# Five slightly wider matmuls at the start of each feed-forward of a two-layer diffusion step

## The chip, the cores and the metric

The program runs on one core of a Trainium2 chip. The metric is the device time of one execution in microseconds; the median of three executions is given. Beside it there is one execution taken with the hardware profiler, which lists each instruction of each engine with its start and duration. PE is TensorE's matmuls, PEld its weight loads, DVE is VectorE, ACT is ScalarE, POOL is GpSimd, SP the engine whose queue issues all DMA transfers here.

## The reference

Two groups of 128 tokens each, a context group and a denoising group, go through two layers of width 2048. A layer is a mixer (latent attention and grouped-query attention in the first, differential attention in the second) and a gated feed-forward with a convolution over positions. The feed-forward, which the change touches, is

```
def conv_ffn(h, w_up, w_conv, b_conv, w_down):
    u = h @ w_up
    up = jnp.pad(u, ((0, 0), (1, 1), (0, 0)))
    u = up[:, :-2] * w_conv[0] + up[:, 1:-1] * w_conv[1] + up[:, 2:] * w_conv[2] + b_conv
    gate, val = u[..., :D_FF], u[..., D_FF:]
    return (jax.nn.silu(gate) * val) @ w_down
```

with D_FF = 5632. All inputs, weights and outputs are float32. Both groups use the same weights, and the kernel keeps their tokens side by side: a row of the activations has NT = 256 columns, 128 of each group.

## The kernel before

Activations lie with features on the 128 partitions and tokens along the free dimension. A product of float32 accuracy is made of three matmuls on rounded operands: each weight block is split by ScalarE and VectorE into a high part wh and a low part wl (`split`, L236, called from `Weights.chunk`, L274), each activation into a high and a low half. The operand hx holds for each of the 16 feature blocks k a row of 512 columns: 256 of the high half, then 256 of the low half.

`gemm` (L323) makes one chunk of output, 128 features by 256 tokens, in one PSUM bank of 512 columns taken from a pool of three, called acc. It walks the input blocks, 16 for an up-projection and 22 for half a down-projection, and for each issues wh times the high half, wh times the low half and wl times the high half. A weight load goes ahead of each matmul. The first matmul of a chunk clears the accumulator (start), the last closes it. So an up-projection chunk is 48 matmuls and a down-projection chunk 66, all 128x256. All of TensorE's instructions go through `placed` (L104, or L107 for transposes), so all have these lines in the profile and are told apart by their tiles.

The feed-forward (`ffn`, L1246) takes 88 up-projection chunks in turn (gate and value of each of the 44 feature blocks), in two halves of 44, each followed by 16 down-projection chunks that add to the residual. `conv` asks the local function product for a chunk. The first three chunks are `ready`: made before, by `modulated` (L666), from an operand that has not been normalised yet and has 258 columns instead of 256 (UW, two of them for the shift). The next four come from the list in_order: they are issued in a fixed order. The third of these four, chunk 5 when counted from 0, has a hook in its middle (turn): four transposes into a bank called misc, which end the computation of a modulation vector. From chunk 7 on in_order is empty and nothing stands between the chunks.

The order on each engine comes from a scheduler with a timeline simulation of its own. Weights come as tiles of 1 MB through SP's queue (raw), three of them in flight, and the split parts wh and wl have four buffers each.

Of the kernel before, what the change touches and what calls it, by code (L numbers as in the profile page):

```python
# [21 lines left out]
NT = 2 * T  # L22
# [32 lines left out]
LATE = 3  # L55

EARLY = (2, 5, 8, 11, 13)
SENT = (1, 3, 6, 9, 12, 14, 16)
FINE = 4

# [28 lines left out]
def step_kernel(ctx: ExitStack, tc: tile.TileContext, A: dict):  # L89
# [4 lines left out]
    def keep_order(i):  # L94
        if not any(i is j for j in kept):
            kept[:] = [i]
            tc.keep_in_program_order(i)
# [16 lines left out]
    pe = TensorE()  # L114
# [11 lines left out]
    def banks(name):  # L126
        return tc.tile_pool(name=name, bufs=1, space=PSUM)
# [7 lines left out]
    def T_(pl, shape, tag, dt=F32, bufs=None):  # L135
        kw = {} if bufs is None else {"bufs": bufs}
        return pl.tile(shape, dt, tag=tag, name=nm(tag), **kw)
# [8 lines left out]
    def C(name):  # L146
        a, w = _AT[name]
        return cst[:, a:a + w]
# [87 lines left out]
    def split(out_hi, out_lo, src, pin=lambda i: i):  # L236
        pin(act.copy(out_hi, src))  # L237
        pin(dve.tensor_tensor(out=out_lo, in0=src, in1=out_hi.bitcast(F32), op=ALU.subtract))  # L238
# [81 lines left out]
            pin(pe.matmul(ps[c][:, :NT], wl, xh(k), start=False, stop=b))  # L320
        return [p[:, :NT] for p in ps]

    def gemm(blocks, xh, xl, n=NT, first=0, between=None):  # L323

        fixed = lambda i: keep_order(i) if between is not None else i
        ps = T_(pacc, [P, 512], "acc")
        last = len(blocks) - 1
        for i in range(last + 1):  # L330
            k = (i + first) % (last + 1)
            wh, wl = blocks[k]
            fixed(pe.matmul(ps[:, :n], wh, xh(k), start=(i == 0), stop=False))
            if callable(between):
                if i == (last + 1) // 2:
                    between()
            elif between and i in between:
                between[i]()
            fixed(pe.matmul(ps[:, :n], wh, xl(k), start=False, stop=False))
            fixed(pe.matmul(ps[:, :n], wl, xh(k), start=False, stop=(i == last)))  # L340
        return ps[:, :n]
# [96 lines left out]
    def load_row():  # L438
        feat["row"] = T_(feat["home"], [P, 2, D], "condb")
        sp.dma_start(out=feat["row"], in_=A["condb"])  # L440
        for r in range(2):
            keep_order(act.activation(feat["row"][:, r], feat["row"][:, r], AF.Silu))
# [118 lines left out]
    def pump(rows, feats=0.0, until=None):  # L561

        until = until or RLIMIT[stage[0]]
        step()
        side_pump()
        ada["due"] += rows
        while ada["due"] >= 0.25:
            if ada["i"] >= until and not later:
                ada["due"] = 0.0
                break  # L570
            ada["due"] -= 0.25 if ada["i"] >= until else 0.25 * ada["pew"]
            row_step(until)
        feat["due"] += feats
        while feat["due"] >= 1.0 and feat["i"] < FLIMIT[stage[0]]:
            feat["due"] -= 1.0
            feature_step()

    def ensure(l, j, qs=range(4)):
        for u in [(l, j, q) for q in qs]:
            while u in ROWS and u not in done and ada["i"] <= ROWS.index(u):  # L580
                row_step()
            while u in FEATS and u not in done:
                feature_step()
            while u not in done:
                later.pop(0)()
# [74 lines left out]
    def operand(pl, tag):  # L660
        return home(pl, tag)[:, :KD * ROW].rearrange("p (k n) -> p k n", k=KD)

    def raw_tile(pl, tag):
        return home(pl, tag)[:, :KD * 2 * UW].rearrange("p (k n) -> p k n", k=KD)
# [580 lines left out]

    def ffn(hx, W, ready, turn, l, st):  # L1246
        xh, xl = (lambda k: hx[:, k, :NT]), (lambda k: hx[:, k, NT:2 * NT])
        product = lambda: ready.pop(0) if ready else gemm(W.chunk(), xh, xl, between=in_order.pop(0) if in_order else None)
        WD = Weights(A["w_down"][l], KQ, TB)
        cw = ada["cw"]  # L1250
        with tc.tile_pool(name=f"ffn{l}", bufs=1) as fp, banks(f"pffn{l}") as pf:
            feat["home"], feat["pool"] = fp, pf
            feat["due"] = 0.0
            in_order = [{}, {}] + turn + [{}]
            T_(fp, [P, SHIFT // 4], "pad")

            def conv(m):
                early = bool(ready)
                pin = keep_order if early else lambda i: i
                ps = product()  # L1260
                y = T_(fp, [P, NT], "cv", bufs=3)
                pin(act.activation(y, ps, AF.Identity, scale=cw[:, 1, m:m + 1], bias=cw[:, 3, m:m + 1]))  # L1262
                y3 = y.rearrange("p (g t) -> p g t", g=2)
                p3 = ps.rearrange("p (g t) -> p g t", g=2)
                pin(dve.scalar_tensor_tensor(out=y3[:, :, 1:], in0=p3[:, :, :T - 1],  # L1265
                                             scalar=cw[:, 0, m:m + 1], in1=y3[:, :, 1:],
                                             op0=ALU.mult, op1=ALU.add))
                pin(dve.scalar_tensor_tensor(out=y3[:, :, :T - 1], in0=p3[:, :, 1:],  # L1268
                                             scalar=cw[:, 2, m:m + 1], in1=y3[:, :, :T - 1],
                                             op0=ALU.mult, op1=ALU.add))  # L1270
                if early and ready:
                    W.ahead(pin)
                return y

            def up(q):
                gs = []
                for i in range(q * KQ, (q + 1) * KQ):
                    rate = 0 if i < LATE else FRATE["up"]
                    fine[0] = False
                    gate = conv(i)  # L1280
                    pump(0, rate)
                    val = conv(NFF + i)
                    pump(0, rate)
                    act.activation(gate, gate, AF.Silu)
                    dve.tensor_tensor(out=val, in0=gate, in1=val, op=ALU.mult)
                    g = T_(fp, [P, ROW], "g", F32R, bufs=KQ)
                    split(g[:, :NT], g[:, NT:2 * NT], val)
                    gs.append(g)
                    if i == LATE - 1:
                        load_row()  # L1290
                return gs

            def down(gs, q):
                u, rows = None, None
                if q == NQ - 1 and l < NL - 1:
                    u = raw_tile(keep, "hx")
                    rows = raw_rows(u, l + 1, 0)
                for c in range(KD):
                    quiet = q == NQ - 1 and c >= KD - QUIET[0]
                    fine[0] = quiet  # L1300
                    if q == 0:
                        ensure(l, 5, [c // 4])
                    ps = gemm(WD.chunk(), lambda k: gs[k][:, :NT], lambda k: gs[k][:, NT:2 * NT])
                    if l == NL - 1 and q == NQ - 1 and c == KD - 1:
                        last_residual(ps, l, 1, c, st)
                    else:
                        residual(ps, l, 1, c, st if q == NQ - 1 else None)
                    if rows:
                        rows(c)
                    if l == NL - 1 and q == NQ - 1 and c in EARLY:  # L1310
                        act.activation(x[:, c], x[:, c], AF.Identity, scale=C("gfin")[:, c:c + 1])
                    pump(0, 0 if quiet else FRATE["down"])
                return u

            for q in range(NQ):
                gs = up(q)
                u = down(gs, q)
            while feat["i"] < FLIMIT[stage[0]]:
                feature_step()
            return u  # L1320


    with banks("pab") as ppool["ada"]:
# [3 lines left out]
        first = {1: load_half(1, 0, "araw"), 0: load_half(0, 0, "raw")}  # L1327
# [6 lines left out]
        hx = operand(keep, "hx")  # L1334
        st = stat_init()
        with tc.tile_pool(name="beside", bufs=1) as beside:
            o = mixer_ab(hx, rb0, beside)
            with tc.tile_pool(name="raw", bufs=1) as rp:
# [3 lines left out]
                W = Weights(A["w_up"][0], KD, 1)  # L1342
# [5 lines left out]
    with tc.tile_pool(name="cc", bufs=1) as cp, banks("pc") as ppool["ada"]:  # L1348
# [3 lines left out]
        W = Weights(A["w_in_c"], KD, 1)  # L1352
# [5 lines left out]
        W = Weights(A["w_up"][1], KD, 1)  # L1358
        hx, *begun = modulated(st, 1, 1, W, u, (keep, "hx"), cp)
    stage[0] = "ffn1"  # L1360
    st = stat_init()
    ffn(hx, W, *begun, 1, st)
    rb = spread(final_rstd(st))
    rbs = T_(tmp, [P, NT], "nt", bufs=4)
    sent = 0
    for c in range(KD):
        if c in EARLY:
            pool.tensor_tensor(out=x[:, c], in0=x[:, c], in1=rbs, op=ALU.mult)
# [3 lines left out]
        if c == 0:  # L1372
            act.copy(rbs, rb)
        if c + 1 in SENT:
            sp.dma_start(out=A["o_y"][:, sent:c + 1], in_=x[:, sent:c + 1])
# [132 lines left out]
```

## Time and profile before

| | |
|---|---|
| median of three executions | 2363.69 us (2362.99 to 2365.67) |
| profiled execution, its own time | 2362.23 us |
| profiled execution, span from first to last instruction | 2360.4 us |
| granted TensorE clock, mean | 0.995 |
| matmuls and weight loads | 19666 each |
| first feed-forward after its turn, on the chain of waits | from 488 to 1178 us |
| second feed-forward after its turn, on the chain of waits | from 1633 to 2348 us |

How the rows in the prediction are read. The page's first part gives for each engine busy microseconds, share of the span and number of instructions. The chain of waits is followed back from the last instruction to what released each step; a row of it has the start in us, the length in us and what ran, with the number of instructions. A row of the timeline has start, length, engine, line, operation, output and inputs, the shape, and how many equal instructions it merges. A row of busy times per stretch names the stretch, its length, and for each engine the busy time and the number of instructions that ran in it, then the granted clock, the DMA share and the rate. Matmuls overlap: one takes 0.28 us from its start to the end of its result, but the next starts 0.11 to 0.12 us after it, so a pace is read from starts or from counts, not from durations.

### The profile page before, as it was taken

How to read it: one execution, taken by the hardware profiler on the slowest of the kernel's cores; microseconds unless marked ns; L12 is line 12 of the kernel's file. 1: busy time of each engine (PE TensorE's matmuls, PEld its weight loads, DVE VectorE, ACT ScalarE, POOL GpSimd, SP SyncE). 2: the span in 40 equal slices, each digit the busy share in tenths (PEclk: the TensorE clock that was granted, in tenths of full speed). 3: DMA queues.
4: the chain of work that ended last, by engine and by line, in shares of the span. 5: the costliest groups of instructions: out<-in, count | busy, mean ns of one | idle time of the engine just before them, and what ended most of it. 6: DMA issues, size and time to landing. Idle time of an engine off the chain costs nothing.

```text
span 2360.4 us, 47894 instructions
## 1 busy us (share of the span) xinstructions
PE 2323.6 (98%) x19666; PEld 2214.8 (94%) x19666; DVE 1850.4 (78%) x2864; ACT 1191.4 (50%) x1980; POOL 176.7 (7%) x242
## 2 busy tenths in 40 slices
PE   6999999999999999999999999999999999999998
PEld 4788778999999999999999999999999999999998
DVE  3569767889989999999988888787998655666644
ACT  4246545665554455555564545557555434555443
POOL 0002101300000000001130000122000000000011
PEclk9999999999999999999999999999999999999999
DMA  9988888677777777677778888667666555555553
GB/s 362 352 327 300 305 321 325 239 281 265 267 259 283 295 271 267 251 263 273 281 279 304 302 293 315 233 249 274 251 250 242 183 193 181 193 181 190 185 185 119
DMA packets 106811, 612.97 MB, mean 260 GB/s; under 512 B 11552, under 2 KB 19552, under 8 KB 38880
## 3 DMA queue, kind: packets, MB, share of 16 engines
q1 hardware_dynamic: 106592, 609.92, 70.8%
q8 instruction: 154, 2.52, 0.4%
q14 instruction: 65, 0.53, 0.1%
HBM read 605.12 MB, written 4.75 MB: 258 GB/s over the span
## 4 chain that ended last, share of the span: by engine, by line
PE 96%; DVE 2%; DMA 1%; ACT 1%; issue 0%; SPq 0%; POOL 0%; DVEq 0%; ACTq 0%
PE acc L104 88%; PE ada L104 4%; PE att L104 2%; PE att L107 1%; PE misc L104 1%; DVE wl L238 1%; DMA araw<-w_ada 0%; PE ada L107 0%; ACT wh L237 0%; DMA raw<-w_in_ab 0%; DVE x L1370 0%; DVE aacc L481 0%; DVE nt L604 0%; DMA block<-w_ada 0%; DVE proj L960 0%
## 5 line engine op out<-in xcount | busy, mean ns | idle before, releaser
L104 PE MATMUL acc<-hx,wh 128*128 128x256 f32 (+1 forms) x7296 | 1280.3, 280 | 5.5 <-ACT hx L614 4.3
L237 ACT CAST wh<-raw 128x1024 fp32r<-128x1024 f32 (+2 forms) x824 | 794.5, 976 | 955.8 <-PE acc L104 760.1
L238 DVE TENSOR_TENSOR wl<-raw,wh 128x1024 fp32r<-128x1024 f32 (+2 forms) x824 | 920.2, 1132 | 309.6 <-ACT wh L237 307.0
L104 PEld LDWEIGHTS acc<-hx,wh 128*128 128x128 f32 x7296 | 1114.0, 189 | 37.9 <-issue 17.2
L104 PE MATMUL acc<-hx,wl 128*128 128x256 f32 (+1 forms) x3648 | 1016.7, 279 | 4.4 <-DVE wl L238 4.4
L104 PEld LDWEIGHTS acc<-hx,wl 128*128 128x128 f32 x3648 | 686.9, 188 | 5.5 <-DVE wl L238 5.5
L104 PE MATMUL acc<-g,wh 128*128 128x256 f32 x2816 | 488.2, 278 | 0.0
L104 PEld LDWEIGHTS acc<-g,wh 128*128 128x128 f32 x2816 | 429.2, 189 | 0.0
L104 PE MATMUL acc<-g,wl 128*128 128x256 f32 x1408 | 391.7, 278 | 0.0
L104 PE MATMUL acc<-hxc,wh 128*128 128x256 f32 (+1 forms) x1536 | 276.6, 281 | 0.0
L452 DVE CUSTOM_DVE_ANT_0 junk<-araw,condb 128x2048 f32<-128x2048 f32 x120 | 275.8, 2299 | 0.0
L104 PEld LDWEIGHTS acc<-g,wl 128*128 128x128 f32 x1408 | 264.2, 188 | 0.0
L104 PEld LDWEIGHTS acc<-hxc,wh 128*128 128x128 f32 x1536 | 235.9, 188 | 8.7 <-issue 8.4
L104 PE MATMUL acc<-hxc,wl 128*128 128x256 f32 (+1 forms) x768 | 213.5, 278 | 0.0
L200 POOL TENSOR_TENSOR sqacc<-sqacc,sq 128x256 f32<-128x256 f32 x62 | 71.1, 1146 | 1539.9 <-ACT sq L196 1533.3
L481 DVE SCALAR_TENSOR_TENSOR aacc<-block,condw,aacc 128x512 f32<-128x512 f32 x240 | 172.1, 755 | 12.4 <-DMA block<-w_ada 12.3
L104 PEld LDWEIGHTS acc<-hxc,wl 128*128 128x128 f32 x768 | 144.5, 188 | 0.3
L104 PE MATMUL ada<-araw,condw 128*32 128x512 f32 (+1 forms) x736 | 91.3, 591 | 12.8 <-DMA araw<-w_ada 12.8
L1262 ACT ACTIVATE cv<-acc,convw 128x256 f32<-128x256 f32 x170 | 95.0, 559 | 0.0
L773 DVE SCALAR_TENSOR_TENSOR x<-acc,mod,x 128x128 f32<-128x128 f32 x190 | 57.4, 344 | 39.7 <-PE acc L104 39.6
L1268 DVE SCALAR_TENSOR_TENSOR cv<-acc,convw,cv 128x254 f32<-128x254 f32 x170 | 81.4, 479 | 3.3
L1265 DVE SCALAR_TENSOR_TENSOR cv<-acc,convw,cv 128x254 f32<-128x254 f32 x170 | 80.8, 475 | 0.0
(229 smaller groups left out, 1400.4 us busy)
## 6 DMA issues: line engine op xcount, KB each, us to landing
raw<-w_up SPq DMA_DIRECT2D x176, 1024.0 KB, 4.8
araw<-w_ada SPq DMA_DIRECT2D x146, 1024.0 KB, 6.0
raw<-w_down SPq DMA_DIRECT2D x88, 1024.0 KB, 4.8
raw<-w_in_c SPq DMA_DIRECT2D x48, 1024.0 KB, 6.9
block<-w_ada SPq DMA_DIRECT2D x128, 256.0 KB, 5.4
raw<-w_in_ab SPq DMA_DIRECT2D x19, 1024.0 KB, 7.1
raw<-w_out_ab SPq DMA_DIRECT2D x16, 1024.0 KB, 7.0
raw<-w_out_c SPq DMA_DIRECT2D x16, 1024.0 KB, 5.8
```

What stands on the lines that cost most here:

```text
L104: return self.placed(nc.tensor.matmul(*a, **kw))
L107: return self.placed(nc.tensor.transpose(*a, **kw))
L200: eng.tensor_tensor(out=st["acc"], in0=st["acc"], in1=sq, op=ALU.add)
L237: pin(act.copy(out_hi, src))
L238: pin(dve.tensor_tensor(out=out_lo, in0=src, in1=out_hi.bitcast(F32), op=ALU.subtract))
L452: keep_order(dve.tensor_tensor_reduce(out=T_(feat["pool"], [P, D], "junk"), in1=feat["row"][:, c], in0=feat["raw"].rearrange("p g n -> p ( ...
L481: i = dve.scalar_tensor_tensor(out=acc[c], in0=block, scalar=condw[:, k, c:c + 1], in1=acc[c], op0=ALU.mult, op1=ALU.add)
L773: dve.scalar_tensor_tensor(out=x[:, c, s], in0=ps[:, s], scalar=mod[:, l, 3 * which + 2, c, g:g + 1], in1=x[:, c, s], op0=ALU.mult, op1=AL ...
L1262: pin(act.activation(y, ps, AF.Identity, scale=cw[:, 1, m:m + 1], bias=cw[:, 3, m:m + 1]))
L1265: pin(dve.scalar_tensor_tensor(out=y3[:, :, 1:], in0=p3[:, :, :T - 1], scalar=cw[:, 0, m:m + 1], in1=y3[:, :, 1:], op0=ALU.mult, op1=ALU.add))
L1268: pin(dve.scalar_tensor_tensor(out=y3[:, :, :T - 1], in0=p3[:, :, 1:], scalar=cw[:, 2, m:m + 1], in1=y3[:, :, :T - 1], op0=ALU.mult, op1=A ...
```

## The change

In each feed-forward a list of five numbers, 32, 16, 8, 4 and 2, is used up by the first five chunks after in_order is empty, chunks 7 to 11. For such a chunk the first matmul, the one that clears the accumulator, reads so many columns more of hx: behind the 256 columns of block 0's high half lie the columns of its low half. It writes as many columns more of the bank. `gemm` still returns the first 256 columns, so the others are not read. All other matmuls keep 256 columns.

```diff
+WIDER = (32, 16, 8, 4, 2)
...
-    def gemm(blocks, xh, xl, n=NT, first=0, between=None):
+    def gemm(blocks, xh, xl, n=NT, first=0, between=None, more=None):
...
-            fixed(pe.matmul(ps[:, :n], wh, xh(k), start=(i == 0), stop=False))
+            x0 = more(k) if more and i == 0 else xh(k)
+            fixed(pe.matmul(ps[:, :x0.shape[-1]], wh, x0, start=(i == 0), stop=False))
...
-        product = lambda: ready.pop(0) if ready else gemm(W.chunk(), xh, xl, between=in_order.pop(0) if in_order else None)
+        wider = list(WIDER)
+
+        def product():
+            if ready:
+                return ready.pop(0)
+            if in_order:
+                return gemm(W.chunk(), xh, xl, between=in_order.pop(0))
+            if wider:
+                n = NT + wider.pop(0)
+                return gemm(W.chunk(), xh, xl, more=lambda k: hx[:, k, :n])
+            return gemm(W.chunk(), xh, xl)
+
```

## The prediction

> **What bounds the kernel now.** First the page: who is busy, and what the chain that ended last consists of.
>
> ```profile
> span 2360.4 us, 47894 instructions
> PE 2323.6 (98%) x19666; PEld 2214.8 (94%) x19666; DVE 1850.4 (78%) x2864; ACT 1191.4 (50%) x1980; POOL 176.7 (7%) x242
> PE 96%; DVE 2%; DMA 1%; ACT 1%; issue 0%; SPq 0%; POOL 0%; DVEq 0%; ACTq 0%
> ```
>
> TensorE carries 96% of the chain, so the time is the number of matmuls times the pace at which they start. Next the chain in order of time, for its long pieces, and the busy times of the same number of microseconds inside each, for the matmuls on acc alone.
>
> ```profile
> 488.02 690.34 PE acc L104 x6090
> 1632.56 715.04 PE acc L104 x6071
> ```
>
> ```profile
> core 0: us, PE busy (x) PEld busy (x) DVE busy (x) ACT busy (x), PEclk, DMA share, GB/s
> 500.00:1170.00 670.00, 670.00 (x5914) 670.00 (x5913) 95.49 (x223) 45.21 (x81) 1.00 0.73 269
> 1650.00:2320.00 670.00, 670.00 (x5691) 670.00 (x5691) 94.05 (x218) 44.78 (x80) 1.00 0.57 203
> ```
>
> These two pieces are the two feed-forwards: the same 6071 matmuls of 128x256 without a gap (23 left of a chunk, 82 chunks of 48, 32 of 66), yet the second takes 25 us more. In 670 us the first starts 5912 matmuls (two of the 5914 were still running from before), one every 113.33 ns; the second 5689, one every 117.77 ns. The granted clock is 1.00 in both. The slower one has less DMA traffic (0.57 against 0.73), so neither clock nor transfers explain the 4.44 ns. Nor does other engines' work:
>
> ```profile
> core 0: us, PE busy (x) PEld busy (x) DVE busy (x) ACT busy (x) POOL busy (x), PEclk, DMA share, GB/s
> 488.00:1178.30 690.30, 690.30 (x6093) 690.30 (x6091) 640.45 (x833) 353.46 (x490) 17.21 (x14) 1.00 0.73 269
> 1632.60:2347.60 715.00, 715.00 (x6074) 715.00 (x6072) 476.78 (x630) 339.42 (x450) 16.51 (x14) 1.00 0.56 197
> ```
>
> VectorE is busier in the fast one (640 us against 477). So the same stream has two cadences, and each feed-forward keeps the one it began with. The next view, busy time in stretches between breaks, shows that these two recur elsewhere (only TensorE's first count matters).
>
> ```profile
> 399.00:408.00 9.00, 9.00 (x79) 9.00 (x78) 0.61 (x2) 0.00 (x0) 1.00 0.92 363
> 1221.00:1230.00 9.00, 9.00 (x79) 9.00 (x78) 0.00 (x0) 0.73 (x2) 1.00 0.80 285
> 1240.00:1249.00 9.00, 9.00 (x82) 9.00 (x82) 0.00 (x0) 0.72 (x2) 1.00 0.64 190
> 1280.50:1289.50 9.00, 9.00 (x79) 9.00 (x79) 0.00 (x0) 0.73 (x2) 1.00 0.90 320
> 1301.00:1310.00 9.00, 9.00 (x82) 9.00 (x81) 0.00 (x0) 0.72 (x2) 1.00 0.88 297
> 1546.00:1555.00 9.00, 9.00 (x82) 9.00 (x81) 1.19 (x4) 0.00 (x0) 1.00 0.95 363
> ```
>
> Nine microseconds hold 82 matmuls or 79, nothing between: 9000/113.33 = 79.4 and 9000/117.77 = 76.4, with two or three carried over. A stretch has one cadence throughout, and a break by other matmuls draws it anew. What the break before the slow feed-forward looks like, in order of time, with the same break in the fast one:
>
> ```profile
> 487.31 0.28 PE L104 MATMUL acc<-hx,wh 128*128 128x256 f32 x1
> 487.42 0.60 PE L107 MATMUL misc<-cst,am 128*128 128x128 f32 x4
> 487.78 0.36 PE L104 MATMUL acc<-hx,wh 128*128 128x256 f32 x1
> 487.98 0.28 PE L104 MATMUL acc<-hx,wl 128*128 128x256 f32 x1
> 488.34 0.28 PE L104 MATMUL acc<-hx,wl 128*128 128x256 f32 x1
> 488.68 0.28 PE L104 MATMUL acc<-hx,wl 128*128 128x256 f32 x1
> ...
> 1631.84 0.28 PE L104 MATMUL acc<-hx,wh 128*128 128x256 f32 x1
> 1631.96 0.60 PE L107 MATMUL misc<-cst,am 128*128 128x128 f32 x4
> 1632.32 0.36 PE L104 MATMUL acc<-hx,wh 128*128 128x256 f32 x1
> 1632.52 0.28 PE L104 MATMUL acc<-hx,wl 128*128 128x256 f32 x1
> 1632.87 0.28 PE L104 MATMUL acc<-hx,wl 128*128 128x256 f32 x1
> 1633.22 0.28 PE L104 MATMUL acc<-hx,wl 128*128 128x256 f32 x1
> ```
>
> Both breaks are the four transposes of turn. The first stream limps (0.36 us from wl to wl, three matmuls), then has 0.34; the second goes straight to 0.35 and stays. My reading: the cadence is a phase lock between the stream and some fixed beat. 113.33 is 17 x 6.667 ns, and three slow matmuls, 353.3 ns, are 53 x 6.667; a beat of 6.667 ns is an estimate from these two rows. A lock is left only if something shifts the phase.
>
> **The change, part by part.** Comparing the two programs' instructions engine by engine, ten rows differ, all on TensorE: in each feed-forward the first matmul of chunks 7 to 11 (counted from 0) has 288, 272, 264, 260 and 258 columns instead of 256. Nothing is moved or added on VectorE, ScalarE, GpSimd or the DMA queues, and no wait: the extra columns of hx are its low half, written long before, and land in a part of the bank that nobody reads.
>
> *Direct price of the columns.* 62 per feed-forward, 124 in all. The nearest rows are the 384-column matmuls:
>
> ```profile
> 248.17 0.34 PE L104 MATMUL acc<-kv_in,wl 128*128 128x384 f32 x1
> 249.21 0.34 PE L104 MATMUL acc<-kv_in,wl 128*128 128x384 f32 x1
> ```
>
> Six matmuls lie between these starts (wl, wh, wh, twice): 173.3 ns each, so 60 ns for 128 columns, 0.47 ns a column. 124 columns are 0.06 us. Nothing hides them: the stream has no gap.
>
> *What a shift does to a lock.* No row shows one wide matmul inside a stream. The nearest are the stages that stream 258 columns throughout, and what follows them.
>
> ```profile
> 1602.27 0.41 PE L104 MATMUL acc<-hxc,wh 128*128 128x258 f32 x2
> 1604.78 0.28 PE L104 MATMUL acc<-hxc,wh 128*128 128x258 f32 x1
> ...
> 1617.86 0.41 PE L104 MATMUL acc<-hxc,wh 128*128 128x258 f32 x2
> 1618.11 0.28 PE L104 MATMUL acc<-hxc,wl 128*128 128x258 f32 x1
> 1618.23 0.40 PE L104 MATMUL acc<-hx,wh 128*128 128x256 f32 x2
> 1618.47 0.28 PE L104 MATMUL acc<-hx,wl 128*128 128x256 f32 x1
> 1618.81 0.28 PE L104 MATMUL acc<-hx,wl 128*128 128x256 f32 x1
> ```
>
> The busy times of the 12 us behind it:
>
> ```profile
> 1618.70:1630.70 12.00, 12.00 (x108) 12.00 (x107) 0.90 (x2) 1.09 (x3) 1.00 0.98 393
> ```
>
> Between the first two lie 21 matmuls in 2.51 us: 119.5 ns each. Two columns more should cost 0.9 ns by the price above; they cost 6.2 over the fast cadence. A shift of 0.9 ns in every matmul thus suffices to keep the stream out of either lock, and when the width returns to 256 the stream is in the fast cadence (0.34 from 1618.47 to 1618.81) after two matmuls and keeps it (108 in 12 us: 106 at 113.33 and two carried over). That is what each wide matmul does once, with shifts of 15, 7.5, 3.8, 1.9 and 0.9 ns: it moves the phase and 47 matmuls of one width follow in which the stream can settle. Against the estimated beat the first two shifts are near whole beats and may leave the phase where it was; the third is half a beat and should move it most. The last, one eighth, decides what remains: the 258-column tail above is its nearest row, and settles fast.
>
> *Gain in the second feed-forward.* 71 matmuls lie between the turn and chunk 7 (23 + 48), so 6000 come from there on: if the first shift frees it, 6000 x 4.44 ns = 26.6 us; the fifth, 192 matmuls later, 25.8. I take the third: 5904 x 4.44 = 26.2 us. Bounds below and above: a loss of nothing (no shift frees it), a gain of 26.6.
>
> *Price in the first feed-forward,* which is fast already: nothing if it settles back, 6000 x 4.44 = 26.6 us if the last shift leaves it slow. I take nothing, by the same row. Settling costs at most what a limping matmul does, 119.5 - 113.3 = 6 ns, for perhaps four matmuls after each of ten shifts: 0.25 us with the columns' own 0.06 rounded in as 0.3.
>
> *Is the rest fast enough?* At 113.33 the second feed-forward asks for weights 4% sooner. The first does so with 640 us of VectorE work against 477 and a DMA share of 0.73 against 0.56, and has no gap in 690 us, so the cover holds.
>
> *Sum.* The profiled execution took 2362.23 us (span 2360.4 and 1.8 around it); 2362.2 - 26.2 + 0.3 = 2336.3. The median of the three runs, 2363.69, lies 1.5 above it: 2337.8. Breaks in the attention layer may draw other cadences; a stretch of 96 matmuls is worth 0.4 us, so I allow some 3 us either way: 2333 to 2341.
>
> **The rivals.**
>
> *No lock is changed, or the two swap.* The wide matmuls only lengthen the stream: 2363.7 + 0.1 = 2363.8. If the first feed-forward turns slow while the second turns fast, the 26s cancel and the time is the same 2364. For it: a lock that survived 6071 matmuls may survive a shift of whole beats, and the small shifts could be swallowed. Against it: 258 columns never lock. [...]
>
> *The shifts free nothing and catch the first feed-forward.* Slower: the fast cadence is lost at 496 us (488.0 + 71 x 0.113) and the second stays slow: 2363.7 + 26.6 = 2390.3. It decides at the last of the five shifts, since later ones can undo what earlier ones did. For it: breaks do end in the slow cadence, three of the six stretches above, and five shifts are five draws. Against it: those breaks are large (other shapes, a pause), and the one tail of two columns shown ended fast.
>
> *A third, limping pace after the shifts* as with 258 columns: 12,000 x 6.2 ns less the second's 26.6: 48 us more, 2411. Only matmuls of unequal width show it, so it is unlikely.
>
> **How the numbers follow.** Both fast 0.72; no change or a swap 0.15; both slow 0.10; other slower 0.03. About 0.2% (4.7 us) is what a measurement of this kernel can tell from no change. So faster 0.72, same 0.15, slower 0.13. The forecast's own range, 2333 to 2341, holds some 0.7; to hold 8 in 10 the range reaches up to no change, 2366. The predicted time is that of the likeliest case, 2337.5.
>
> **What would show it.** In the changed profile the second long piece of the chain should be 690 us instead of 715, with 5912 matmuls in 670 us from 1650 on, and the slow pace should end at one of the five wide matmuls, between 1641 and 1664 us; I expect the 264-column one. The first piece should stay 690 us. I am wrong if the count in the second stays at 5689 (no lock left), or if that in the first falls to it (the shift catches as easily as it frees).

## The result and the profile after

The changed kernel took 2337.22 us (median of four runs, 2334.74 to 2339.60) against 2364.68 us before (four runs, 2362.99 to 2366.09): a ratio of 0.9886, 95% interval 0.9874 to 0.9899. That is 27.5 us less. The page of the profiled execution (2337.88 us) begins:

```profile
span 2336.0 us, 47894 instructions
PE 2298.1 (98%) x19666; PEld 2188.7 (94%) x19666; DVE 1850.7 (79%) x2864; ACT 1193.6 (51%) x1980; POOL 177.0 (8%) x242
```

As many instructions of every engine as before; only TensorE is busy for a shorter time, 25.5 us. Where it became shorter is seen in the chain of waits in order of time (start, length, what; the kernel's lines are shifted, so L105 is what L104 was):

```profile
488.54 690.47 PE acc L105 x6090
...
1634.57 688.68 PE acc L105 x6071
```

The first feed-forward kept its time, 690.47 us against 690.34; the second fell from 715.04 to 688.68, by 26.36. The span fell by 24.4 only, because the second feed-forward began 2.0 us later than before (1634.57 against 1632.56). Of these 2.0 us, 0.5 had passed before the first feed-forward and 0.1 went by in it. The rest lies between the two feed-forwards, where the change has nothing: that stretch takes 454.2 to 456.3 us in the traces of this case, 454.2 before and 455.6 here. The medians differ by 1.1 us more than the second feed-forward gained, which is within the scatter of the four executions on each side.

The busy times in the same two stretches as before, and then stretches between the wide matmuls of the second feed-forward (matmuls on acc alone; TensorE's first count is what matters):

```profile
500.00:1170.00 670.00, 670.00 (x5913) 670.00 (x5912) 95.11 (x222) 45.27 (x81) 1.00 0.73 269
1650.00:2320.00 670.00, 670.00 (x5913) 670.00 (x5913) 96.15 (x224) 45.24 (x81) 1.00 0.57 205
...
1635.00:1642.00 7.00, 7.00 (x62) 7.00 (x61) 1.75 (x4) 0.56 (x1) 1.00 0.72 243
1643.20:1648.20 5.00, 5.00 (x44) 5.00 (x44) 0.95 (x2) 0.56 (x1) 1.00 0.58 190
1649.00:1653.50 4.50, 4.50 (x42) 4.50 (x41) 0.48 (x2) 0.57 (x1) 1.00 0.22 62
1654.50:1659.00 4.50, 4.50 (x42) 4.50 (x41) 0.47 (x1) 0.56 (x1) 1.00 0.44 137
1659.80:1664.30 4.50, 4.50 (x42) 4.50 (x41) 0.57 (x2) 0.55 (x1) 1.00 0.67 224
1665.40:1669.90 4.50, 4.50 (x42) 4.50 (x41) 0.95 (x2) 0.56 (x1) 1.00 1.02 411
```

In 670 us both feed-forwards now start about as many matmuls; the second had 5691. The short stretches show where it changed. Up to the 288-column matmul at 1642.8 us and after it the pace is still slow: 7 us hold 59.4 matmuls at 117.77 ns and 5 us hold 42.5, with about two carried over. From the 272-column matmul on it is fast: 4.5 us hold 39.7 at 113.33. The remaining three leave it fast. The timeline at that place:

```profile
1647.97 0.28 PE L105 MATMUL acc<-hx,wl 128*128 128x256 f32 x1
1648.32 0.28 PE L105 MATMUL acc<-hx,wl 128*128 128x256 f32 x1
1648.44 0.41 PE L105 MATMUL acc<-hx,wh 128*128 128x272 f32 x2
1648.68 0.28 PE L105 MATMUL acc<-hx,wl 128*128 128x256 f32 x1
1649.03 0.28 PE L105 MATMUL acc<-hx,wl 128*128 128x256 f32 x1
1649.37 0.28 PE L105 MATMUL acc<-hx,wl 128*128 128x256 f32 x1
```

From wl to wl, three matmuls, it is 0.35 us, then 0.36 across the wide one, 0.35 once more while the stream settles, and 0.34 from there to the end.

### The profile page after: what moved, and what is told of

Same layout as the page of the kernel before. It is cut to its first block, busy times and chain, and to the rows that moved or that the text cites. A ratio compares the mean times of both kernels' runs of the same rounds, so it can differ in the third digit from the quotient of the medians.

```text
span 2336.0 us, 47894 instructions
## 1 busy us (share of the span) xinstructions
PE 2298.1 (98%) x19666; PEld 2188.7 (94%) x19666; DVE 1850.7 (79%) x2864; ACT 1193.6 (51%) x1980; POOL 177.0 (8%) x242
## 4 chain that ended last, share of the span: by engine, by line
PE 95%; DVE 2%; DMA 2%; ACT 1%; issue 0%; SPq 0%; POOL 0%; DVEq 0%; ACTq 0%
PE acc L105 86%; PE ada L105 4%; PE att L105 2%; DMA araw<-w_ada 1%; PE att L108 1%; DVE wl L239 1%; DMA block<-w_ada 1%; PE misc L105 1%; PE ada L108 0%; DVE aacc L483 0%; DMA raw<-w_in_ab 0%; ACT wh L238 0%; DVE x L1383 0%; DVE nt L606 0%; DVE ql L879 0%
## 5 line engine op out<-in xcount | busy, mean ns | idle before, releaser
L105 PE MATMUL acc<-hx,wh 128*128 128x256 f32 (+1 forms) x7296 | 1263.9, 278 | 6.3 <-ACT hx L616 4.3
L105 PEld LDWEIGHTS acc<-hx,wh 128*128 128x128 f32 x7296 | 1104.8, 188 | 38.6 <-issue 15.5
L105 PE MATMUL acc<-hx,wl 128*128 128x256 f32 (+1 forms) x3648 | 1010.5, 277 | 4.5 <-DVE wl L239 4.5
L105 PEld LDWEIGHTS acc<-hx,wl 128*128 128x128 f32 x3648 | 686.8, 188 | 5.6 <-DVE wl L239 5.5
L105 PE MATMUL acc<-g,wh 128*128 128x256 f32 x2816 | 478.9, 276 | 0.0
L105 PEld LDWEIGHTS acc<-g,wh 128*128 128x128 f32 x2816 | 423.7, 188 | 0.0
L105 PE MATMUL acc<-g,wl 128*128 128x256 f32 x1408 | 388.2, 276 | 0.0
L105 PE MATMUL acc<-hxc,wh 128*128 128x256 f32 (+1 forms) x1536 | 276.4, 281 | 0.0
L105 PEld LDWEIGHTS acc<-g,wl 128*128 128x128 f32 x1408 | 264.2, 188 | 0.0
L105 PEld LDWEIGHTS acc<-hxc,wh 128*128 128x128 f32 x1536 | 235.9, 188 | 8.7 <-issue 8.4
L105 PE MATMUL acc<-hxc,wl 128*128 128x256 f32 (+1 forms) x768 | 213.4, 278 | 0.0
L105 PEld LDWEIGHTS acc<-hxc,wl 128*128 128x128 f32 x768 | 144.4, 188 | 0.3
L105 PE MATMUL ada<-araw,condw 128*32 128x512 f32 (+1 forms) x736 | 91.3, 591 | 13.2 <-DMA araw<-w_ada 13.2
```

The source lines that it names most:

```text
L105: return self.placed(nc.tensor.matmul(*a, **kw))
```

## The experiments

All kernels below have the changed kernel's code; the edits are to its list of widths or to where it is used. Times are of one execution each unless an interval is given, and single executions scatter: the kernel before took 2360.2 to 2369.4 us in the seven runs beside the last group. So the verdicts rest on counts, as above: about 5914 matmuls in 670 us are the fast cadence, 5691 the slow one.

### In which feed-forward is it gained?

```diff
-        wider = list(WIDER)
+        wider = list(WIDER) if l == 1 else []     # "second"; l == 0 in "first"
```

> All five widths, in the second feed-forward alone. Theory that the gain is made where the slow stream is: 2337 us, 5913 matmuls in 670 us in the second, 5913 in the first. Rival, the five in the first feed-forward matter, because they change when everything behind them begins: 2364 us, 5691 in the second.

> All five widths, in the first feed-forward alone. Theory that the gain is made in the second: 2364 us, 5691 matmuls in 670 us in the second and 5913 in the first. Rival, a shift in the first changes the second's start: 2337 us, 5913 in both.

Measured: 2340.12 us with the widths in the second alone, 2369.14 with the widths in the first alone; the kernel before took 2367.60 beside them. The stretch from 1650 to 2320 us, first in "second", then in "first":

```profile
1650.00:2320.00 670.00, 670.00 (x5914) 670.00 (x5913) 96.04 (x224) 45.14 (x81) 1.00 0.58 206
```

```profile
1650.00:2320.00 670.00, 670.00 (x5691) 670.00 (x5690) 94.24 (x217) 45.45 (x81) 1.00 0.57 203
```

The gain is made inside the slow stream. The shifts in the first feed-forward did not change the pace of the second.

### Which width frees a slow stream?

One wide matmul, always the first of chunk 7, in both feed-forwards. The stream reaches it slow in the second and fast in the first, so one run tests both.

```diff
-WIDER = (32, 16, 8, 4, 2)
+WIDER = (32,)
```

and the same with 24, 16, 12, 8, 4 and 2.

> Only the first of the five widths, 288 columns, in chunk 7 of both feed-forwards. Lock theory (a cadence holds until the phase is shifted, and 13.3 ns are two whole beats of 6.667 ns): the second feed-forward stays slow as it did behind this matmul in the changed kernel, about 5691 matmuls in 670 us from 1650 on, and the whole takes 2364 us; the first stays at about 5913. Rival, any disturbance frees a slow stream: 5913 in both, 2337 us.

> Only 272 columns, in chunk 7 of both. In the changed kernel the slow stream ended behind the 272-column matmul, with a 288-column one before it. Theory that this width alone does it: 5913 matmuls in 670 us in both feed-forwards, 2337 us. Theory that the 288 columns had to move the three-matmul pattern first (it stood one matmul further behind them): the second stays at 5691, 2364 us. Theory of whole beats (6.7 ns is one beat, so nothing moves): also 5691, 2364 us.

> Only 264 columns, half a beat, in chunk 7 of both. Lock theory with a 6.667 ns beat: the largest shift of the five, so the second feed-forward is freed, 5913 matmuls in 670 us and 2337 us; the first returns to the fast cadence as it did in the changed kernel, 5913. Rival, only 272 columns free it: 5691 in the second, 2364 us. Rival, a single shift can also catch the fast stream: first at 5691, 2364 to 2391 us.

> Only 260 columns, a quarter of a beat, in chunk 7 of both. Lock theory: freed if a quarter of a beat leaves the slow lock's basin, 5913 in the second and 2337 us; if the lock pulls it back, 5691 and 2364 us. The first stays at 5913 either way, as behind the 260-column matmul of the changed kernel. Rival, only 272 columns free it: 5691, 2364 us.

> Only 258 columns, an eighth of a beat (0.9 ns), in chunk 7 of both. If the tail of the 258-column stage in the kernel before is the right neighbour, 2 columns free the slow stream: 5913 matmuls in 670 us in the second feed-forward, 2337 us. If the slow lock pulls so small a shift back: 5691 and 2364 us. First feed-forward 5913 either way.

> Only 280 columns (24 more, a beat and a half by the 6.667 ns estimate) in chunk 7 of both feed-forwards. Beat theory: what counts is the shift modulo the beat, so it acts like 8 columns and frees the slow stream, though 16 and 32 alone did not: 5914 matmuls in 670 us in the second feed-forward, 2338 us. Rival, small shifts free and large ones do not, because a long matmul lets the weight loads catch up: 5691, 2366 us.

> Only 268 columns (12 more, three quarters of a beat) in chunk 7 of both. Beat theory: a shift of minus a quarter, by symmetry with 4 columns outside the slow lock's basin: 5914 in the second feed-forward, 2338 us. If the basin is one-sided, the stream is pulled back: 5691, 2366 us. First feed-forward 5914 either way.

Measured, with the number of columns counted in sixteenths of the estimated beat (16 columns are put at 6.7 ns; in the trace the start behind the 272-column matmul came 7 to 8 ns later):

| extra columns | beats | time, us | second feed-forward, was slow | first feed-forward, was fast |
|---|---|---|---|---|
| 2 | 1/8 | 2367.69 | stays slow | stays fast |
| 4 | 1/4 | 2339.94 | fast | stays fast |
| 8 | 1/2 | 2337.16 | fast | stays fast |
| 12 | 3/4 | 2336.81 | fast | stays fast |
| 16 | 1 | 2361.85 | stays slow | stays fast |
| 24 | 1 1/2 | 2367.78 | fast | turns slow |
| 32 | 2 | 2365.81 | stays slow | stays fast |

The rows of the second feed-forward, one kernel each, in the order 2, 4, 8, 12, 16 and 32:

```profile
1650.00:2320.00 670.00, 670.00 (x5691) 670.00 (x5690) 93.71 (x216) 45.35 (x81) 1.00 0.57 203
```

```profile
1650.00:2320.00 670.00, 670.00 (x5914) 670.00 (x5913) 96.19 (x224) 45.15 (x81) 1.00 0.58 206
```

```profile
1650.00:2320.00 670.00, 670.00 (x5915) 670.00 (x5914) 96.21 (x224) 45.10 (x81) 1.00 0.58 205
```

```profile
1650.00:2320.00 670.00, 670.00 (x5914) 670.00 (x5913) 96.08 (x224) 44.61 (x80) 1.00 0.58 205
```

```profile
1650.00:2320.00 670.00, 670.00 (x5691) 670.00 (x5691) 94.02 (x217) 44.86 (x80) 1.00 0.57 203
```

```profile
1650.00:2320.00 670.00, 670.00 (x5691) 670.00 (x5690) 93.82 (x216) 45.30 (x81) 1.00 0.57 202
```

What frees the stream is not the size of the shift but its part of 16 columns: 4, 8, 12 and 24 do, 16 and 32 do not. Each width stood alone in one kernel, 264 columns in two more below. That excludes a rule by which small shifts act and large ones don't, or the other way round, and it is what a beat of 16 columns gives. The extra columns as such, read from the low half and written behind the result, are excluded too, since 16 and 32 do the same. Across the 272-column matmul alone the timeline of the 16-column kernel shows a pure delay:

```profile
1639.91 0.28 PE L105 MATMUL acc<-hx,wl 128*128 128x256 f32 x1
1640.27 0.28 PE L105 MATMUL acc<-hx,wl 128*128 128x256 f32 x1
1640.39 0.41 PE L105 MATMUL acc<-hx,wh 128*128 128x272 f32 x2
1640.63 0.28 PE L105 MATMUL acc<-hx,wl 128*128 128x256 f32 x1
1640.98 0.28 PE L105 MATMUL acc<-hx,wl 128*128 128x256 f32 x1
1641.34 0.28 PE L105 MATMUL acc<-hx,wl 128*128 128x256 f32 x1
```

0.36 us across it, and 0.35 or 0.36 ever after, 117.77 ns each.

The starts in the traces are kept to one nanosecond and show more than these rows. A line at the known pace through 30 starts before the wide matmul, and another through 30 starts shortly behind it, give the delay that stays. In the fast stream it was 20.0 ns for 2 columns, 13.3 for 4, 20.1 for 8, 26.7 for 12, 33.3 for 16 and 46.7 for 32: three, two, three, four, five and seven times 6.667, though the very next start came only 2 to 14 ns later. So a stream that kept the fast pace was delayed by whole beats in every case. In the slow stream it was 6.7 ns, one beat, for 2 columns and for 16, so 2 columns made it skip a beat without freeing it. For 32 columns it was 11.1 ns, a beat and two thirds.

In the changed kernel, as in "second", the 272 columns freed the stream, but there the 288-column matmul stood before it, with the same delay of 11.1 ns, and had left the pace as slow as it was. A slow matmul lasts 17 2/3 beats, so a slow stream is at the same point of the beat at every third start only; behind the 288 columns it was two thirds of a beat away from where it had been. That the 272-column matmul acts in the one position and not in the other for this reason is inferred from these runs; no run put it at the third position.

The 24-column kernel gave the other half of the question. Its chain:

```profile
493.46 717.02 PE acc L105 x6090
...
1664.76 688.41 PE acc L105 x6071
```

It freed the second feed-forward and caught the first: 717.02 + 688.41 = 1405.43 us, against 690.34 + 715.04 = 1405.38 before. The swap among the rivals exists, and a fast stream is not safe from a shift.

### Is it a shift, or just more work at that place?

```diff
-WIDER = (32, 16, 8, 4, 2)
+WIDER = (0,)
...
-            fixed(pe.matmul(ps[:, :x0.shape[-1]], wh, x0, start=(i == 0), stop=False))
+            for r in range(2 if more and i == 0 else 1):
+                fixed(pe.matmul(ps[:, :x0.shape[-1]], wh, x0, start=(i == 0), stop=bool(more and i == 0 and r == 0)))
```

> The five wide matmuls are gone; instead chunk 7 of each feed-forward issues its first matmul twice at 256 columns. Theory that a shift by a part of the beat is needed: one more matmul of the same width is one more step of the same pattern, so the second feed-forward stays slow, about 5691 in 670 us, 2364 us. Rival, any additional work at that place resets the pace: 5913, 2337 us.

Measured: 2367.56 us, and in the second feed-forward

```profile
1650.00:2320.00 670.00, 670.00 (x5691) 670.00 (x5690) 93.69 (x216) 45.25 (x81) 1.00 0.57 203
```

One matmul more, 118 ns, does nothing to the pace; 4 columns, some 2 ns, end it. Additional work as such is excluded.

### Does the gain begin where the shift is?

```diff
-WIDER = (32, 16, 8, 4, 2)
+WIDER = (0,) * 53 + (8,)
```

> 264 columns, but in chunk 60 of both feed-forwards instead of chunk 7. Lock theory: the second stays slow for 53 chunks of 48 matmuls more, 2544 x 4.44 ns = 11.3 us, so 2338 + 11.3 = 2349 us, with the change of pace some 300 us behind the place it had. Rival, the whole feed-forward is set by its first microseconds and a late shift comes too late or finds another pattern: 2366 us.

Measured: 2350.44 us. The chain's piece and the two sides of the wide matmul, which is at 2063 us:

```profile
1631.43 704.40 PE acc L105 x6071
```

```profile
1700.00:2060.00 360.00, 360.00 (x3059) 360.00 (x3059) 48.88 (x114) 23.56 (x42) 1.00 0.59 208
2065.00:2325.00 260.00, 260.00 (x2296) 260.00 (x2295) 36.28 (x86) 15.85 (x29) 1.00 0.54 187
```

360 us hold 3057 matmuls at 117.77 ns, 260 us hold 2294 at 113.33, again with two carried over. So a stream that has been slow for 430 us is freed at the place of the shift. The first feed-forward got the same shift in its chunk 60 and stayed fast (5914 matmuls in 670 us). The piece is 16.0 us longer than the 688.4 of the kernels with the same width in chunk 7, where 11.3 was expected. The expectation had counted 53 chunks of 48 and forgotten the 16 down-projection chunks of 66 that lie between chunks 43 and 44: (2544 + 1056) x 4.44 ns = 16.0 us.

### Is one wide matmul enough?

```diff
-WIDER = (32, 16, 8, 4, 2)
+WIDER = (8,)
...
-        wider = list(WIDER)
+        wider = list(WIDER) if l == 1 else []
```

> One wide matmul in all: 264 columns in chunk 7 of the second feed-forward alone. If that is all the change needs: ratio 0.989 to the kernel before, as for the five widths in both (0.9886), and 2338 us. If the other nine add something: above 0.990.

Measured: a ratio of 0.9901, interval 0.9878 to 0.9924, 2338.16 us. The interval holds both the ratio of the changed kernel and the bound that was set, so the time does not tell one from ten. The profile does as far as it goes: in the profiled execution the second feed-forward is fast behind that one matmul (5907 matmuls in 670 us from 1650 on, with the end of the stage inside), as with ten. No version beat the changed kernel beyond the scatter.

## Why the prediction was right, point by point

*What bounds the kernel.* Held. TensorE's pace was what changed, and the time followed it. The prediction called the two long pieces the same 6071 matmuls, but the first has 6090: its last 19 are 258-column matmuls of the next layer. Its first 6071 starts span 688.0 us, so the two paces are 27 us apart over equal work, not 25, and the second piece came at 688.68 and not at the 690 that was named as the sign.

*Two cadences, kept until the phase is shifted.* Held, and shown: by the extra matmul that does nothing, by the shift in chunk 60 that acts there, and by widths that act by their part of 16 columns. That the beat is 6.667 ns was an estimate; the delays in whole multiples of it measure it, and the seven widths agree with a period of 16 columns for the slow stream. What part of TensorE has this beat is open. "Nothing between" 79 and 82 left out a stretch of the same answer: 418 to 427 us holds 81, and its starts are 113.33 ns apart, so it is fast as well. And these breaks do not draw the cadence by chance: in all fourteen traces the first feed-forward begins fast and the second slow.

*The direct price.* All ten shifts were put at 0.3 us. The first feed-forward, which was fast before and after, grew by 0.13 us for its five, the sum of the delays above; twice that is 0.26. The columns' own 0.47 ns each were the smaller part of it, as the prediction had it; the rest went by while the stream settled, whole beats later.

*The gain.* 26.2 us was forecast for the second feed-forward, 26.36 came: 715.04 to 688.68. Chunk by chunk it adds up as the prediction counted it, with the second shift instead of the third as the one that frees: 5952 matmuls x 4.44 ns = 26.4 us.

*Which shift frees.* Wrong. The prediction took the 264-column matmul, since two shifts of whole beats should leave the phase alone. The first left the pace alone but not the phase, which moved by a beat and two thirds. The second moved a slow stream by one whole beat when it stood alone, and freed it behind the first. The 264-column matmul does free the stream when it stands alone, so the forecast had a sound ground, but not the one that acted.

*The last shift decides, and 2 columns are enough.* Wrong, and the forecast came out only because it was not needed. The tail of the 258-column stage was taken as the nearest row for one matmul of 258 columns. But there every matmul had shifted the phase and the stream was in no lock when the width returned; here it sits in the slow one, and 2 columns alone left it there, one beat later. That row shows no more than a stream out of both locks that settled fast; the 24-column kernel has one that settled slow.

*The price in the first feed-forward.* Nothing was taken, and that is what came. The same row was the reason, and it is weaker than it looked: at six of the seven widths the fast stream came back, at 24 columns it turned slow, at a price of 717.02 - 690.34 = 26.7 us, the 26.6 of the rival. That the five widths of the change are not among those that catch was luck.

*The rivals.* No lock changed: excluded here, though it is what 2, 16 or 32 columns alone would have given. The Trainium skill, page TensorE: Matmul & The Clock Gate, section Back-to-back issue gap, gives N/2.4 + 2.5 ns as the warm gap of an isolated matmul, a formula in its columns alone, and says that in a stream with weight loads both operations set the spacing. It has no second pace for the same stream, which these runs show: 24 columns in each feed-forward moved each of them by some 27 us, in opposite directions. The swap and the caught first feed-forward are real outcomes at another width. A lasting third pace was not seen in a feed-forward of any run.

*Is the rest fast enough?* Held: the second feed-forward at 113.33 ns has no gap, at a DMA share of 0.57.

*The sum.* It gives 2337.8 us, while the last figure of the prediction is 2337.5; nothing on record accounts for the 0.3. That the time came within 0.3 us of the forecast is in part luck: the kernel before took 2364.68 in this comparison, 1.0 more than the sum started from, and the medians fell by 27.5 where 25.9 had been forecast.

## What to carry to other kernels

Where a long stream of equal matmuls has no gap, count its starts over some hundred microseconds and compare stages of equal shape: two paces with the same clock and less other work on the slower one pointed here to a lock, not to a resource. A shift by a few columns at one matmul cost 13 to 47 ns in the fast stream and changed the pace of everything up to the next break, so it is worth trying where the stretch behind it is long. One matmul of 264 columns freed the slow stream in all three kernels that had it alone; whether several different shifts in a row are surer than one was not tested. Check the streams that were fast as well: the same means can make them slow, and the total then hides both.

## What was not expected of the hardware

Of equal shifts modulo 16 columns, the slow stream takes 8 and 24 alike, both free it, but the fast stream does not: 8 columns leave it fast, 24 make it slow (690.36 against 717.02 us for the same 6090 matmuls). And the state survives long: 3600 slow matmuls after chunk 7 passed without a change before the shift in chunk 60 ended them.
